# Attention value products: the column halves of the array hold two softmax rows in place of two halves of the key blocks, and one transpose turns two heads' sums

## Chip, cores and metric

The kernel runs on one core of one Trainium2 chip. The metric is the device time of one execution in microseconds (us), lower is better. Engines are written as in the profile: PE is TensorE (PEld its weight loads), DVE is VectorE, ACT is ScalarE, POOL is GpSimd.

## What is computed

Two layers of a hybrid diffusion backbone over 1024 latent tokens and 256 context tokens of width 1024, all in float32. In each layer one input projection feeds four head groups of four heads of 64 (A: global attention with two key/value heads, B: attention in a band of 128 tokens to each side, with a sink, also two key/value heads, C: an mLSTM, D: attention in a 2-D neighbourhood with a learned bias, four key/value heads). Their outputs are normalised by group, go through one output projection, and a gated MLP follows. The change touches the end of A, B and D alone, the weighted sum of values and its division:

```python
p = jax.nn.softmax(s, axis=-1).astype(vals.dtype)
return jnp.einsum('bkgqs,bksd->bkgqd', p, vals)
...
y = rms_norm(y.reshape(b, t, N_GROUPS, GROUP_WIDTH), g_group.reshape(N_GROUPS, GROUP_WIDTH))
```

## The kernel before

**Stages of a layer.** `phase1` normalises, projects for A and runs attention A (`attn_a`), with the rest of the projections (`pj`, lines 111 to 113) behind it. `attn_d` runs D, with the mLSTM steps as filler, and hands on to `attn_b`, which finishes B, with the first part of the output projection (`o`) as filler. `phase3` does the rest of the output projection and the MLP (`b`).

**Jobs.** A query tile has 128 tokens. `job_a` and `job_b` make one job for each tile and key/value head, so two softmax rows (the two query heads that share it); `job_d` makes one for a pair of tiles and one head, so two rows as well (the two tiles). Layer 0 treats 10 tiles, layer 1 only the 8 latent ones. `run_jobs` interleaves the generator `one` of a job (scores, softmax) with `two` of the jobs before it (products, division), and `pump` puts filler between them. That is the order in which instructions are handed over; a scheduler with a simulated timeline then sets the final order of each engine's queue at compile time, by readiness and by that order.

**Scores and softmax.** In A (`job_a`) scores are made with keys on the partitions, so E (exponentials, written two key blocks at a time at line 1136) can go into the products directly. In B and D (`softmax_rows`) queries are on the partitions, and `weigh` first transposes the probabilities cell by cell (a cell is one row and one key block of 128 keys), four cells to a PSUM tile `pT` (line 976), copied to `PT` by ACT or DVE (lines 982, 980).

**Products.** The values of a key block (128 keys by 64) are the weights, the probabilities stream through. Such a product uses 64 of the array's 128 columns, and it is made in one column half, the next product in the other (`r = HD * half`). In the kernel before, a product streams both rows of a block at once (256 columns), blocks alternate between the halves, and so the sum O (128 x 256) has the even blocks' part in partitions 0 to 63 and the odd blocks' part in 64 to 127. In A this is line 1151 (10 key blocks a job, 2 for context tiles). In `weigh` it is line 965, called for one group of at most four cells, one group after the transposes of the next. Products are float32, and the profile has two records for each, two passes.

**Division.** O is copied to `Os` (lines 1155, 1200, 1339). `finish_y` multiplies each head's 128 x 128 slice with two identities stacked (`self.ii`, 128 x 64, line 1006), which adds the two parts and turns the result to tokens on partitions in one product. Line 999 turns the order of D's denominators (`back`), line 1003 sums A's. Then `rd` (line 1008) and `yu` (line 1010) divide, and `group_norm` writes the result.

Of the kernel before, what the change touches and what calls it, by code (L numbers as in the profile page):

```python
# [7 lines left out]
F32 = mybir.dt.float32  # L8
F32R = mybir.dt.float32r
BF16 = mybir.dt.bfloat16  # L10
AF = mybir.ActivationFunctionType
# [4 lines left out]
P = 128  # L16
# [6 lines left out]
HD = 64  # L23
# [16 lines left out]
    return ap.bitcast(F32)  # L40


NB = (3, 4, 4)

SLOTS = "gwwwwgggwwwwggggwww"
# [2 lines left out]
class Net:  # L48
# [893 lines left out]
    def weigh(self, rows, blocks, V, take):  # L942


        nc = self.nc
        yield
        groups = [[]]
        for b in blocks:
            cells = [(s, b) for s in range(2) if b in rows[s][1]]
            if len(groups[-1]) + len(cells) > 4:  # L950
                groups.append([])
            groups[-1] += cells
        O = None
        late = []

        def products(cells, pt):
            nonlocal O, half
            if O is None:
                O = self.asp.tile([P, 256], F32, tag="O", name="O", bufs=1)
            c = 0  # L960
            while c < len(cells):
                s, b = cells[c]
                n = 2 if c + 1 < len(cells) and cells[c + 1][1] == b else 1
                r = HD * half
                nc.tensor.matmul(O[r:r + HD, s * P:(s + n) * P], V[b], pt[:, c:c + n].rearrange("p s t -> p (s t)"),  # L965
                                 start=(cells is groups[0]), stop=(cells is groups[-1]), skip_group_check=True)
                half = 1 - half
                c += n

        half = 0  # L970
        for cells in groups:
            n = len(cells)
            t = self.asp.tile([P, 4, P], F32, tag="T", name="pT", bufs=2)
            for c, (s, b) in enumerate(cells):
                Pm, col = rows[s]
                nc.tensor.transpose(t[:, c], Pm[:, col[b]:col[b] + P], self.ident)  # L976
            pt = self.ap_.tile([P, 4, P], F32, tag="PT", name="PT", bufs=3)
            self.turn += 1
            if self.turn % 4 == 0:
                nc.vector.tensor_copy(pt[:, 0:n], t[:, 0:n])  # L980
            else:
                nc.scalar.copy(out=pt[:, 0:n], in_=t[:, 0:n])
            late.append((cells, pt))
            if len(late) > 1:
                products(*late.pop(0))
            yield cells is groups[-1]
        yield True
        products(*late.pop(0))
        take(O)
        yield True  # L990

    def finish_y(self, i, grp, Os, den, wp, back=False, sums=None):


        nc = self.nc
        Yt = self.asp.tile([P, 4, P], F32, tag="T", name="Y", bufs=2).rearrange("p a b -> p (a b)")
        Y = Yt[:, 0:256]
        if back:
            nc.tensor.matmul(Yt[:, 256:260], self.back, den, start=True, stop=True)
            den = Yt[:, 256:260]  # L1000
        if sums:
            for h in range(4):
                nc.tensor.matmul(Yt[:, 256 + h:257 + h], sums[h // 2][:, 0, h % 2], self.ones[:, 0:1], start=True, stop=True)
            den = Yt[:, 256:260]
        for h in range(4):
            nc.tensor.matmul(Y[:, h * HD:(h + 1) * HD], Os[h], self.ii, start=True, stop=True)  # L1006
        rd = wp.tile([P, 4], F32, tag="rd", name="rd")
        nc.vector.reciprocal(rd, den)
        yu = wp.tile([P, 256], F32, tag="yu", name="yu", bufs=1)
        nc.vector.tensor_tensor(out=yu.rearrange("p (h d) -> p h d", d=HD), in0=Y.rearrange("p (h d) -> p h d", d=HD),  # L1010
                                in1=rd.unsqueeze(2).broadcast_to([P, 4, HD]), op=ALU.mult)
        self.group_norm(yu, i, grp, wp)

    def attn_pools(self, st, name, side, q_bufs, qt_bufs):
        p = {"qp": self.sb(st, name + "q", bufs=q_bufs, side=side), "wp": self.sb(st, name + "w", bufs=2, side=side)}
        p["ii"] = p["wp"].tile([P, HD], F32, name="ii", bufs=1)
        self.nc.sync.dma_start(p["ii"], self.a["ii"])
        p["ap_"] = self.sb(st, name + "p", side=side)
        p["qt_bufs"] = qt_bufs
        return p  # L1020
# [72 lines left out]
    def job_a(self, i, kv, t, KS, VS, fetch, prep):  # L1093

        nc = self.nc
        blocks = range(2 if i < 2 else NT)
        n = len(blocks)

        def one():
# [33 lines left out]
            for b in range(0, n, 2):  # L1133
                e = E[:, b:b + 2]
                nc.vector.tensor_tensor(out=e, in0=e, in1=T[:, 2:4].unsqueeze(1).broadcast_to([P, 2, 2, P]), op=ALU.subtract)
                nc.scalar.activation(out=e, in_=e, func=AF.Exp)
                if b:
                    nc.gpsimd.tensor_tensor(D, E[:, 0:2] if b == 2 else D, e, ALU.add)
                yield
# [5 lines left out]
        def two():  # L1145
            E = t["E", kv]
            yield
            O = self.asp.tile([P, 256], F32, tag="O", name="O", bufs=1)
            for b in blocks:
                r = HD * (b % 2)  # L1150
                nc.tensor.matmul(O[r:r + HD], VS[:, b, kv], E[:, b].rearrange("p h t -> p (h t)"),  # L1151
                                 start=(b < 2), stop=(b >= n - 2), skip_group_check=True)
            if kv == 0:
                t["Os"] = self.wp.tile([P, 4, P], F32, tag="Os", name="Os", bufs=1)
            nc.scalar.copy(out=t["Os"][:, 2 * kv:2 * kv + 2], in_=O.rearrange("p (s t) -> p s t", s=2))
            yield True
            if kv:
                self.finish_y(i, 0, [t["Os"][:, h] for h in range(4)], None, self.wp, sums=t["ds"])
                yield True
        return dict(one=one, two=two)  # L1160

    def job_b(self, i, kv, t, KS, VS, mask, sink, fetch, prep):
# [33 lines left out]

        def take(O):
            if kv == 0:
                t["Os"] = self.wp.tile([P, 4, P], F32, tag="Os", name="Os", bufs=1)
            nc.scalar.copy(out=t["Os"][:, 2 * kv:2 * kv + 2], in_=O.rearrange("p (s t) -> p s t", s=2))  # L1200

        def two():
            yield from self.weigh(t["rows", kv], blocks, {b: VS[:, b, kv] for b in blocks}, take)
            if kv:
                den = t["den"]
                nc.vector.tensor_tensor(out=den, in0=den, in1=t["es"], op=ALU.add)
                self.finish_y(i, 1, [t["Os"][:, h] for h in range(4)], den, self.wp)
                yield True
        return dict(one=one, two=two)

# [76 lines left out]
    def job_d(self, pair, h, t, KS, VS, EP, EI, fetch, prep):  # L1287
# [21 lines left out]

        def one():  # L1310
            if h == 0:
                for s in range(2):
                    t["den", s] = self.wp.tile([P, 4], F32, tag=f"den{s}", name="den")
            if h == 1:
                fetch((pair[0] + 2, pair[0] + 3))
            if h == 3:
                prep((pair[0] + 2, pair[0] + 3))
            t["rows", h] = []
            for s in range(2):
                r0, nr, bias = info[s]  # L1320
                chunks = [(K[:, 0:NCTX], None)]
                if nr:
                    n = nr * HD // 2
                    bf = bias.rearrange("p a b -> p (a b)")
                    for c in range(2):
                        k0 = NCTX + r0 * HD + c * n
                        chunks.append((K[:, k0:k0 + n], bf[:, c * n:(c + 1) * n]))

                def after(Pm, nm, nr=nr):
                    if nr == 9:  # L1330
                        nc.gpsimd.memset(Pm[:, 832:896], 0.0)

                Pm = yield from self.softmax_rows(chunks, (*t["q"][s], h), 3.0e38, t["den", s][:, h:h + 1], 896, after)
                t["rows", h].append((Pm, cols[s]))

        def take(O):
            if h == 0:
                t["Os"] = self.wp.tile([P, 4, 2, P], F32, tag="Os", name="Os", bufs=1)
            nc.scalar.copy(out=t["Os"][:, h], in_=O.rearrange("p (s t) -> p s t", s=2)[:, :, ::-1])

        def two():
            yield from self.weigh(t["rows", h], blocks, {b: VS[:, b, h] for b in blocks}, take)
            if h == 3:
                for s in range(2):
                    self.finish_y(pair[s], 3, [t["Os"][:, x, s] for x in range(4)], t["den", s], self.wp, True)
                    yield True
        return dict(one=one, two=two)


# [320 lines left out]
def constants():  # L1670
# [1 line left out]
    c = {}  # L1672
    c["ident"] = np.eye(P, dtype=f)
    c["back"] = np.ascontiguousarray(np.eye(P, dtype=f)[::-1])
    c["ii"] = np.concatenate([np.eye(HD, dtype=f)] * 2)
    s8 = np.zeros((P, 8), f)
    for g in range(4):
        for v in range(2):
# [62 lines left out]
```

## Time and profile before

| what | value |
|---|---|
| median of three runs | 3477.2 us (3476.16 to 3477.77) |
| the profiled execution's own time | 3473.32 us |
| its span in the trace | 3471.6 us |
| mean granted TensorE clock | 0.976 |
| busy, share of the span | PE 96%, PEld 78%, DVE 63%, ACT 43%, POOL 28% |
| matmul records | 19629 |

The span is the time from the first to the last instruction of the profiled execution; the own time has what lies around it too. Busy shares are means over stages that differ. A matmul's record is longer than the time after which the next one may start, since matmuls are pipelined: what a matmul costs is read from one start to the next.

### The profile page before, as it was taken

How to read it: one execution, taken by the hardware profiler on the slowest of the kernel's cores; microseconds unless marked ns; L12 is line 12 of the kernel's file. 1: busy time of each engine (PE TensorE's matmuls, PEld its weight loads, DVE VectorE, ACT ScalarE, POOL GpSimd, SP SyncE). 2: the span in 40 equal slices, each digit the busy share in tenths (PEclk: the TensorE clock that was granted, in tenths of full speed). 3: DMA queues.
4: the chain of work that ended last, by engine and by line, in shares of the span. 5: the costliest groups of instructions: out<-in, count | busy, mean ns of one | idle time of the engine just before them, and what ended most of it. 6: DMA issues, size and time to landing. Idle time of an engine off the chain costs nothing. (4 is left out here: it accounts for less than half of the span.)

```text
span 3471.6 us, 52832 instructions
## 1 busy us (share of the span) xinstructions
PE 3332.2 (96%) x19629; PEld 2698.5 (78%) x19629; DVE 2178.5 (63%) x4103; ACT 1498.5 (43%) x3005; POOL 967.1 (28%) x1069
## 2 busy tenths in 40 slices
PE   7999999999988999999999999999999889999998
PEld 4777877777867888888888678877778668888887
DVE  4545553775457778778454736654763588888745
ACT  4334423566544444444120535434564444444321
POOL 1524333232353222220000623424222543322000
PEclk8999999999998999999999999999999989999999
DMA  7645145315321222216222543156233222222521
GB/s 281 184 133 170 41 118 152 87 59 173 125 81 58 73 66 65 74 60 221 75 83 73 160 162 101 44 139 153 60 127 108 83 73 76 91 76 103 195 84 61
DMA packets 393897, 377.52 MB, mean 109 GB/s; under 512 B 118184, under 2 KB 335400, under 8 KB 387496
## 3 DMA queue, kind: packets, MB, share of 16 engines
q1 hardware_dynamic: 393640, 374.15, 34.1%
q8 instruction: 155, 2.54, 0.3%
q14 instruction: 102, 0.84, 0.1%
HBM read 279.69 MB, written 94.37 MB: 108 GB/s over the span
## 5 line engine op out<-in xcount | busy, mean ns | idle before, releaser
L112 PE MATMUL b<-g,w 128*128 128x512 f32 (+1 forms) x880 | 321.9, 368 | 0.0
L113 PE MATMUL b<-g,w 128*128 128x512 f32 (+1 forms) x880 | 320.8, 368 | 0.0
L111 PE MATMUL b<-g,w 128*128 128x512 f32 (+1 forms) x880 | 320.1, 368 | 0.0
L1638 DVE SCALAR_TENSOR_TENSOR xT<-b,modT,xT 128x512 f32<-128x512 f32 (+1 forms) x280 | 191.5, 695 | 202.9 <-PE b L113 202.3
L111 PE MATMUL pj<-whi,hh 128*128 128x512 f32 (+2 forms) x800 | 282.0, 355 | 16.9 <-ACT v L528 7.1
L112 PE MATMUL pj<-wlo,hh 128*128 128x512 f32 (+2 forms) x800 | 281.5, 353 | 2.8 <-DVE wlo L103 2.7
L113 PE MATMUL pj<-whi,hl 128*128 128x512 f32 (+2 forms) x800 | 278.2, 350 | 0.0
L1512 POOL TENSOR_TENSOR s<-raw 128x512 f32<-128x512 f32 x88 | 120.0, 1363 | 466.1 <-DVE w L1519 387.5
L111 PEld LDWEIGHTS pj<-whi,hh 128*128 128x128 f32 x800 | 153.3, 192 | 52.2 <-ACT v L528 11.1
L111 PEld LDWEIGHTS b<-g,w 128*128 128x128 f32 x880 | 165.5, 189 | 27.8
L112 PEld LDWEIGHTS b<-g,w 128*128 128x128 f32 x880 | 165.6, 189 | 27.4
L113 PEld LDWEIGHTS b<-g,w 128*128 128x128 f32 x880 | 165.3, 188 | 27.6
L112 PEld LDWEIGHTS pj<-wlo,hh 128*128 128x128 f32 x800 | 153.9, 193 | 32.1 <-DVE wlo L103 7.6
L1518 ACT CAST w<-s 128x512 fp32r<-128x512 f32 x176 | 107.0, 618 | 153.2 <-PE b L113 101.9
L113 PEld LDWEIGHTS pj<-whi,hl 128*128 128x128 f32 x800 | 153.7, 192 | 23.5 <-issue 4.7
L1541 DVE SCALAR_TENSOR_TENSOR cg<-u,vec,cg 128x512 f32<-128x512 f32 (+1 forms) x176 | 166.2, 988 | 9.1 <-ACT cg L1536 9.1
L86 ACT CAST w<-raw 128x512 fp32r<-128x512 f32 x88 | 53.7, 619 | 270.5 <-PE b L113 244.1
L1519 DVE TENSOR_TENSOR w<-raw,w 128x512 fp32r<-128x512 f32 x154 | 132.7, 875 | 53.3 <-ACT w L1518 50.3
L112 PE MATMUL o<-yl,wohi 128*128 128x256 f32 x576 | 164.9, 287 | 0.7 <-DVE yl L87 0.7
L113 PE MATMUL o<-yh,wolo 128*128 128x256 f32 x576 | 165.0, 288 | 0.0
L111 PE MATMUL o<-yh,wohi 128*128 128x256 f32 x576 | 164.7, 288 | 0.2
L103 POOL TENSOR_TENSOR wolo<-raw,wohi 128x512 fp32r<-128x512 f32 x80 | 103.9, 1300 | 162.6 <-ACT wohi L102 158.0
(364 smaller groups left out, 9769.4 us busy)
## 6 DMA issues: line engine op xcount, KB each, us to landing
wmod<-in_w_mod_dram SPq DMA_DIRECT2D x48, 1024.0 KB, 6.5
raw<-in_w_up_dram SPq DMA_DIRECT2D x176, 256.0 KB, 2.9
raw<-in_w_down_dram SPq DMA_DIRECT2D x88, 256.0 KB, 4.6
raw<-in_w_in_dram SPq DMA_DIRECT2D x80, 256.0 KB, 4.2
raw<-in_w_out_dram SPq DMA_DIRECT2D x80, 256.0 KB, 3.3
sG<-cv SPq DMA_DIRECT2D x22, 640.0 KB, 3.3
graw<-sG SPq DMA_DIRECT2D x22, 640.0 KB, 5.1
sG<-cv SPq DMA_DIRECT2D x22, 512.0 KB, 4.1
```

The source lines that it names most:

```text
L86: nc.scalar.copy(out=hi, in_=src)
L103: eng.tensor_tensor(lo[:, 0:w], raw[:, 0:w], f32v(hi[:, 0:w]), ALU.subtract)
L111: nc.tensor.matmul(out, lh, rh, start=(first and i == 0), stop=False, **kw)
L112: nc.tensor.matmul(out, lh, rl, start=False, stop=False, **kw)
L113: nc.tensor.matmul(out, ll, rh, start=False, stop=(last and i == n - 1), **kw)
L1512: nc.gpsimd.tensor_tensor(s, x, y, op)
L1518: nc.scalar.copy(out=hi, in_=src)
L1519: nc.vector.tensor_tensor(out=lo, in0=src, in1=f32v(hi), op=ALU.subtract)
L1541: nc.vector.scalar_tensor_tensor(out=o[:, x0:x1], in0=u[:, x0 - d - c:x1 - d - c], scalar=self.cw[w][:, j:j + 1], in1=o[:, x0:x1], op0=ALU ...
L1638: nc.vector.scalar_tensor_tensor(out=xs, in0=o[:, 0:t1 - t0], scalar=modT[:, 40 + f, v:v + 1], in1=xs, op0=ALU.mult, op1=ALU.add)
```

## The change

A product now streams one row of one block (128 columns), the first row into partitions 0 to 63 and the second into 64 to 127, so O is 128 x 128 and each half holds a complete sum. In A, one more thing is new: the first product of a job is made to wait for the last exponential of that job (`add_manual_dep`). In `weigh`, cells are cut in fours across blocks, the products of two groups are issued together after the transposes of a third, the rest at the end, and `PT` has four buffers, not three. `finish_y` transposes a pair of heads at a time; for D the new `finish_pair` transposes one head of both tiles at a time, into one PSUM tile for the two, and takes a second tile of the same ring for the denominators. The division itself is moved to `divide`, unchanged. The constant `ii` and its loads are gone.

```diff
 # weigh
-        groups = [[]]
-        for b in blocks:
-            cells = [(s, b) for s in range(2) if b in rows[s][1]]
-            if len(groups[-1]) + len(cells) > 4:
-                groups.append([])
-            groups[-1] += cells
+        cells = [(s, b) for b in blocks for s in range(2) if b in rows[s][1]]
+        ends = [[c for c in cells if c[0] == s] for s in range(2)]
+        ends = {x[0] for x in ends}, {x[-1] for x in ends}
+        groups = [cells[g:g + 4] for g in range(0, len(cells), 4)]
...
-        def products(cells, pt):
-            nonlocal O, half
+        def products(groups):
+            nonlocal O
             if O is None:
-                O = self.asp.tile([P, 256], F32, tag="O", name="O", bufs=1)
-            c = 0
-            while c < len(cells):
-                s, b = cells[c]
-                n = 2 if c + 1 < len(cells) and cells[c + 1][1] == b else 1
-                r = HD * half
-                nc.tensor.matmul(O[r:r + HD, s * P:(s + n) * P], V[b], pt[:, c:c + n].rearrange("p s t -> p (s t)"),
-                                 start=(cells is groups[0]), stop=(cells is groups[-1]), skip_group_check=True)
-                half = 1 - half
-                c += n
+                O = self.asp.tile([P, P], F32, tag="O", name="O", bufs=1)
+            for cells, pt in groups:
+                for c, x in enumerate(cells):
+                    r = HD * x[0]
+                    nc.tensor.matmul(O[r:r + HD], V[x[1]], pt[:, c], start=(x in ends[0]), stop=(x in ends[1]),
+                                     skip_group_check=True)
...
-            pt = self.ap_.tile([P, 4, P], F32, tag="PT", name="PT", bufs=3)
+            pt = self.ap_.tile([P, 4, P], F32, tag="PT", name="PT", bufs=4)
...
-            if len(late) > 1:
-                products(*late.pop(0))
+            if len(late) > 2:
+                products(late[:2])
+                late = late[2:]
             yield cells is groups[-1]
         yield True
-        products(*late.pop(0))
+        products(late)
         take(O)
 # finish_y
-        Y = Yt[:, 0:256]
-        if back:
-            nc.tensor.matmul(Yt[:, 256:260], self.back, den, start=True, stop=True)
-            den = Yt[:, 256:260]
+        for p in range(2):
+            nc.tensor.transpose(Yt[:, p], Os[:, p], self.ident)
...
-        for h in range(4):
-            nc.tensor.matmul(Y[:, h * HD:(h + 1) * HD], Os[h], self.ii, start=True, stop=True)
+    def finish_pair(self, pair, grp, Os, den, wp):
+        nc = self.nc
+        Yt = self.asp.tile([P, 4, P], F32, tag="T", name="Y", bufs=2).rearrange("p a b -> p (a b)")
+        for h in range(4):
+            nc.tensor.transpose(Yt.rearrange("p (s h d) -> p h s d", s=2, h=4)[:, h], Os[:, h], self.ident)
+        dt = self.asp.tile([P, 4, P], F32, tag="T", name="dT", bufs=2)
+        nc.tensor.matmul(dt[:, 0, 0:8], self.back, den, start=True, stop=True)
+        for s in range(2):
+            self.divide(pair[s], grp, Yt[:, 256 * s:256 * s + 256], dt[:, 0, 4 * s:4 * s + 4], wp)
 # job_a
-                nc.scalar.activation(out=e, in_=e, func=AF.Exp)
+                t["exp", kv] = nc.scalar.activation(out=e, in_=e, func=AF.Exp)
...
-            O = self.asp.tile([P, 256], F32, tag="O", name="O", bufs=1)
+            O = self.asp.tile([P, P], F32, tag="O", name="O", bufs=1)
+            first = True
             for b in blocks:
-                r = HD * (b % 2)
-                nc.tensor.matmul(O[r:r + HD], VS[:, b, kv], E[:, b].rearrange("p h t -> p (h t)"),
-                                 start=(b < 2), stop=(b >= n - 2), skip_group_check=True)
+                for h in range(2):
+                    r = HD * h
+                    m = nc.tensor.matmul(O[r:r + HD], VS[:, b, kv], E[:, b, h], start=(b == 0), stop=(b == n - 1),
+                                         skip_group_check=True)
+                    if first:
+                        self.tc.add_manual_dep(m.ins, t["exp", kv].ins.name, SYNC, reason="all products in one run")
+                    first = False
...
-            nc.scalar.copy(out=t["Os"][:, 2 * kv:2 * kv + 2], in_=O.rearrange("p (s t) -> p s t", s=2))
+            nc.scalar.copy(out=t["Os"][:, kv], in_=O)
 # job_d
-            nc.scalar.copy(out=t["Os"][:, h], in_=O.rearrange("p (s t) -> p s t", s=2)[:, :, ::-1])
+            nc.scalar.copy(out=t["Os"][:, h], in_=O[:, ::-1])
...
-                for s in range(2):
-                    self.finish_y(pair[s], 3, [t["Os"][:, x, s] for x in range(4)], t["den", s], self.wp, True)
-                    yield True
+                self.finish_pair(pair, 3, t["Os"], t["den"], self.wp)
+                yield True
```

## Rows read from the trace of the kernel before

**Rows 1.** Page, busy time by engine (share of the span, records).

```profile
PE 3332.2 (96%) x19629; PEld 2698.5 (78%) x19629; DVE 2178.5 (63%) x4103; ACT 1498.5 (43%) x3005; POOL 967.1 (28%) x1069
```

**Rows 2.** Busy us by stretch, sum of 158 to 456 and 2012 to 2267 (A).

```profile
sum 553.00, PE 549.51 PEld 437.88 DVE 308.06 ACT 246.05 POOL 201.18; mean PE 274.75 PEld 218.94 DVE 154.03 ACT 123.03 POOL 100.59
```

**Rows 3.** Same view, sum of 594 to 754 and 2390 to 2545 (D).

```profile
sum 315.00, PE 311.54 PEld 238.64 DVE 235.34 ACT 182.85 POOL 95.69; mean PE 155.77 PEld 119.32 DVE 117.67 ACT 91.42 POOL 47.84
```

**Rows 4.** Same view, sum of 754 to 901 and 2545 to 2657 (B).

```profile
sum 259.00, PE 253.48 PEld 191.91 DVE 146.90 ACT 175.09 POOL 55.52; mean PE 126.74 PEld 95.95 DVE 73.45 ACT 87.55 POOL 27.76
```

**Rows 5.** Waits, total us, times, longest: ACT in A, DVE in D (layer 0).

```profile
ACT E L1117 <- PE S L1116: 60.6, 40, 4.1
...
DVE Pm L931 <- PE S L930: 11.0, 17, 1.6
```

**Rows 6.** O: records, ns min/median/max, starts, forms; what PE idled for (us, times).

```profile
L965 PE MATMUL O<-PT,vs x784: 272/379/689, 594.0 to 2653.0; 128*64 128x256 f32 x180, 128*64 128x128 f32 x16
L1151 PE MATMUL O<-E,vs x656: 379/379/431, 171.1 to 2267.1; 128*64 128x256 f32 x164
...
  ACT E L1136: 1.9, 5
```

**Rows 7.** Timeline of PE in A: start us, us, instruction.

```profile
2173.15 0.28 PE L111 MATMUL pj<-hh,whi 128*128 128x256 f32 x1
2173.26 0.28 PE L112 MATMUL pj<-hl,whi 128*128 128x256 f32 x1
2173.47 1.95 PE L1151 MATMUL O<-E,vs 128*64 128x256 f32 x16
2175.35 0.38 PE L113 MATMUL pj<-hh,wlo 128*128 128x256 f32 x1
2175.58 0.28 PE L111 MATMUL pj<-hh,whi 128*128 128x256 f32 x1
```

**Rows 8.** Timeline of PE: first and last of A's 131 runs of products.

```profile
171.08 0.65 PE L1151 MATMUL O<-E,vs 128*64 128x256 f32 x4
171.66 0.44 PE L1127 MATMUL mT<-ident,M 128*128 128x128 f32 x2
...
2266.81 0.65 PE L1151 MATMUL O<-E,vs 128*64 128x256 f32 x4
```

**Rows 9.** Timeline of PE: first and last of the 207 runs in D and B.

```profile
594.04 0.98 PE L965 MATMUL O<-PT,vs 128*64 128x256 f32 x4
...
2652.76 0.65 PE L965 MATMUL O<-PT,vs 128*64 128x256 f32 x4
```

**Rows 10.** Timeline of PE: a pair of 128-column products; a 256-column product without partner.

```profile
671.89 0.44 PE L965 MATMUL O<-PT,vs 128*64 128x128 f32 x4
672.26 0.66 PE L976 MATMUL pT<-ident,Pm 128*128 128x128 f32 x4
...
883.94 0.65 PE L965 MATMUL O<-PT,vs 128*64 128x256 f32 x2
884.52 0.66 PE L976 MATMUL pT<-ident,Pm 128*128 128x128 f32 x4
```

**Rows 11.** Records that write or read Y, columns as in the group on O.

```profile
L1006 PE MATMUL Y<-ii,Os x432: 217/275/472, 182.6 to 2656.5; 128*128 128x64 f32 x144
L999 PE MATMUL Y<-den,back x36: 168/253/274, 618.2 to 2552.1; 128*128 128x4 f32 x36
...
L1010 DVE TENSOR_TENSOR yu<-Y,rd x54: 410/424/426, 186.4 to 2656.8; 128x256 f32<-128x256 f32 x54
```

**Rows 12.** Timeline of PE: one tile's eight Y records; two transposes.

```profile
430.55 1.08 PE L1006 MATMUL Y<-ii,Os 128*128 128x64 f32 x8
431.44 0.36 PE L1115 MATMUL S<-QH,ks 128*128 128x256 f32 x1
...
180.82 0.38 PE L1127 MATMUL mT<-ident,M 128*128 128x128 f32 x2
181.03 0.28 PE L1003 MATMUL Y<-ones,D 128*128 128x1 f32 x2
```

## Prediction before the run

> **What bounds the kernel now.** I read the page first: PE is busy 96% of the span [rows 1]. That alone says little, so I cut the span into the stretches that hold the products. In A (553 us over both layers) PE is busy for 549.5 us, in D for 311.5 of 315, in B for 253.5 of 259, while DVE stands at 308, 235 and 147 us and ACT at 246, 183 and 175 [rows 2 to 4]. The waits say the same: ACT stands 60.6 us in layer 0's A for scores that PE has not made, DVE 11.0 us in D [rows 5]. In these three stretches the queue of PE sets the pace, so what counts is how long each PE instruction holds up the next. That is read from starts in the timeline.
>
> **What a run of products costs.** I call products that follow one another in PE's queue a run. A run of 16 records takes 1.88 us to the next instruction [rows 7], one of 4 records 0.58 us [rows 8]. Records come in pairs, one in each column half, so 6 more pass pairs cost 1.30 us: 0.217 us for a pass pair of 256 columns. With 128 columns, 4 records take 0.37 us [rows 10], 0.105 us less for each pass pair, so 0.112 us. The rest is paid once a run. Inside it: 1.88 - 8 x 0.217 = 0.14 us. Ahead of it: O starts 0.21 us after the projection before it, where projections follow each other after 0.11 us, so 0.10 us. Behind it: the second projection comes 0.23 us after the first, so 0.11 us more. Together **0.35 us for each run**, however long.
>
> **Products of A.** Before: 656 records [rows 6] are 328 pass pairs x 0.217 = 71.2 us, and 131 runs [rows 8] x 0.35 = 45.9 us: 117.1 us. Each run is short because exponentials land two key blocks at a time, and the scheduler puts each two products where their exponentials are ready. After: twice the products, each of 128 columns, the two rows of a block in the two halves: 656 pass pairs x 0.112 = 73.5 us. The new wait lets none start before all inputs are there. There are 18 tiles x 2 = 36 jobs, so 36 runs if none is broken. I take 45, as instructions handed over earlier can become ready in mid-run: 15.8 us. The gain is 117.1 - 89.3 = **27.8 us**.
>
> **The wait in A.** The first product now waits for the job's last exponential, and scores of the next job and projections are queued behind it on PE. Now PE idles 1.9 us for exponentials, 5 times [rows 6]. At worst each of 36 jobs waits as long (0.4 us): 14 us; at best nothing, and the 1.9 us are won. I take 2 us, since the queue's order is made for the new wait too. The sum O is done later: 20 pass pairs x 0.112 = 2.2 us behind the last exponential, where the last 4 records took 0.58 us. That delays `Os`, Y and the release of E by 1.7 us; PE has projections to fill it, so I price it at nothing. Without them it would be 36 x 1.7 = 60 us.
>
> **Products of D and B.** Before: 784 records in 207 runs [rows 6, 9]. The code makes 208 groups of cells (48 + 44 in B, 60 + 56 in D), so a group was a run and hardly one was broken. Of the products, 24 are the last two cells of a B job with five key blocks: a 256-column product with no partner, which takes the 0.58 us of a full pair [rows 10]. So 336 pass pairs of 256 columns, 48 such passes alone, 32 pass pairs of 128 columns: 384 x 0.217 + 32 x 0.112 = 86.9 us, and 207 x 0.35 = 72.5 us. After: 752 cells, one pass pair each: 84.2 us. By the code B has 60 runs and D 68 (two groups together, then the rest); I take 63 and 72, so 47.3 us. The gain is 159.4 - 131.5 = **27.9 us**: 14.0 in D, 13.9 in B.
>
> **Turning the sums.** `finish_y`'s 432 records [rows 11] take 0.89 us for a tile's eight [rows 12], 0.111 us each, 48.0 us. After: one transpose for each pair of heads and tile, 108, at 0.21 / 2 = 0.105 us [rows 12], say 0.11: 11.9 us. That is a gain of **36 us**, 12 each in A, B and D. The `back` products halve from 36 records [rows 11] to 18: 2 us.
>
> **Edits priced at nothing.** `Os` copies become half as wide; ACT is not the bound. The fourth `PT` and the loss of `ii` and of its six loads cost no engine time. `divide` is as it was. `finish_pair` holds both tiles of the ring that transposes use through two divisions, nine times: each has 0.42 us of `yu` [rows 11] and as much again at most for the rest, so from nothing to 9 x 1.7 = 15 us. I take nothing by itself, because scores and mLSTM steps do not use that ring; it is one reason for the discount below.
>
> **The sum.** PE is freed of 39.9 us in A, 28.1 in D and 26.0 in B: 94.0 us. In A nothing else is near its limit (DVE 56%), so all but the 2 us of waits shorten the span: 38. In D, DVE would rise from 75% to 235 / 287 = 82%, in B ACT from 68% to 175 / 233 = 75% [rows 3, 4], with chains of dependent steps through both. There I count 80%: 22.5 + 20.8 us. That makes 81 us: 3392 against the profiled execution's own 3473.3 us (span 3471.6), and, as the median of the runs lies 3.9 us above it, **3396 us** as the forecast.
>
> **A rule against it.** The six further pass pairs of the long run add only their columns: 256 columns cost 0.217, 128 cost 0.112, so with 0.105 us for each 128 columns some 0.007 us are left over, and the weight loads of passes after the first are hidden [rows 7, 8, 10]. The Trainium skill ("TensorE: Matmul & The Clock Gate", Part 3, The mechanism) says that a weight load overlaps running matmuls only where the row groups differ; both column halves share them, so each pass would pay its load, an estimated 53 ns for 64 columns by the same page. By that rule the 1408 pass pairs after would cost 75 us more, and the sum would be some 3460 us. The runs of 256 columns here speak against the rule. No row shows a third pass of 128 columns, in which a load has half the time to hide.
>
> **Rivals.** (1) *DVE in D and ACT in B become the bound* and half of the 54 us there is lost: 3477.2 - 38 - 27 = 3412 us. For it: the chains and the shared ring. Against it: both mostly wait for PE today [rows 5]. (2) *The runs stay short.* The scheduler's simulated time knows no price of 0.35 us, so it may put other work between products, and 338 runs remain. Only turning (38 us) is gained: at nine tenths 3442 us. Against it: where products were ready together, 207 runs came of 208 groups. (3) *Slower: loads show in every 128-column pass.* Place: the second half of each run. At most the 0.14 us inside a run is such a load, paid by 1408 pass pairs: 205 us, so 3477 - 81 + 205, about 3600 us. It decides from 81 / 1408 = 58 ns a pass; above, the kernel is slower. Against it: 0.007 us left over above, and the 0.37 us of the four-record run has room for one load only.
>
> **How the numbers follow.** Forecast 0.62, rival 1 0.17, rival 2 0.11, rival 3 0.05 (half of it at a price below 58 ns, still faster), and 0.05 for an order of the queues that costs otherwise. The low end: all 94 us, another 6 for unbroken runs (16 x 0.35), and half of the 12.6 us that PE idles in the three stretches: 3371 us. The high end takes in rivals 1 and 2: 3442 us. About 0.2% is what a measurement of this kernel tells from no change. Faster by more: 0.94; within: 0.02; slower: 0.04.
>
> **What would show it.** Right: products of 128 columns alone, some 180 runs; long runs in A with 0.22 us for two pass pairs; Y with 108 transposes 0.11 us apart; A 38 us shorter over both layers, D and B 20 us each; PE still the busiest in all three. Rival 1: the same PE rows, but PE idle in D behind DVE or in B behind ACT. Rival 2: about as many runs as now. Rival 3: pass pairs more than 0.15 us apart. The forecast is wrong if A does not shorten though its runs did, or if PE waits for exponentials by tens of us.

## Result, and the profile after

The change made the kernel faster, by far less than forecast: 3448.17 us median (3444.78 to 3449.32) against 3477.48 us for the kernel before on the same chip, a ratio of 0.9912 (95% interval 0.9897 to 0.9927). A second measurement in a later session gave 3451.95 us, ratio 0.9927 (0.9914 to 0.9941). That is a gain of 25 to 31 us where 81 were forecast, and outside the range. The profiled execution took 3447.27 us with a span of 3445.1 us, at a mean granted clock of 0.972.

The page's busy time by engine, after (before: [rows 1]):

```profile
PE 3273.5 (95%) x20663; PEld 2734.2 (79%) x20663; DVE 2175.4 (63%) x4103; ACT 1485.1 (43%) x3005; POOL 963.3 (28%) x1069
```

PE is busy for 59 us less, yet the span is only 26.5 us shorter. More than half of what PE was freed of has become idle time: 139.4 us before, 171.6 after. The products and transposes after, from the groups by tile (columns as in [rows 6, 11]):

```profile
L962 PE MATMUL O<-PT,vs x1504: 272/273/477, 575.3 to 2623.8; 128*64 128x128 f32 x188
L1158 PE MATMUL O<-E,vs x1312: 272/273/476, 163.5 to 2221.4; 128*64 128x128 f32 x188
...
L993 PE MATMUL Y<-ident,Os x72: 270/272/477, 173.3 to 2626.8; 128*128 128x128 f32 x72
L1006 PE MATMUL Y<-ident,Os x36: 270/273/329, 598.6 to 2523.7; 128*128 128x128 f32 x36
```

All products have 128 columns, 2816 records or 1408 pass pairs, and 72 + 36 = 108 records turn the sums in place of 432. So the change does what it says. Its unit prices are in the timeline of PE (start us, us, instruction), which also shows the place where the time is lost:

```profile
163.55 0.66 PE L1158 MATMUL O<-E,vs 128*64 128x128 f32 x8
164.13 0.39 PE L114 MATMUL pj<-hh,wlo 128*128 128x256 f32 x1
...
2219.30 2.40 PE L1158 MATMUL O<-E,vs 128*64 128x128 f32 x40
2221.63 0.39 PE L112 MATMUL pj<-whi,hh 128*128 128x256 f32 x1
...
2233.16 1.05 PE L621 MATMUL gt<-ident,gates 128*10 128x128 f32 x8 [0.21 <-DVE X L623]
2252.18 0.44 PE L661 MATMUL tp<-ident,ends 10*4 10x10 f32 x8 [17.98 <-DVE ends L653]
...
2257.85 0.58 PE L113 MATMUL pj<-wlo,hh 128*128 128x256 f32 x1 [3.64 <-DVE wlo L104]
...
2264.14 1.87 PE L711 MATMUL tk<-sel,cum 42*128 42x20 f32 x8
...
2402.45 0.66 PE L962 MATMUL O<-PT,vs 128*64 128x128 f32 x8
```

A job's 40 records of A stand in one run and take 2221.63 - 2219.30 = 2.33 us to the next instruction, 8 records take 0.58 us. So 16 more pass pairs cost 1.75 us, 0.109 us each (forecast 0.112). In D and B most runs are still of 8 records, one group of four products. The four rows from `gt` on are the surprise: between the last transposes of the mLSTM's gates (`gt`) and the transposes of the scans' ends (`tp`) PE does nothing for 18 us, then waits 3.6 us more for a weight. In the kernel before, projections stood there and `tp` did not wait, as its own timeline shows at the same place:

```profile
2293.45 1.05 PE L620 MATMUL gt<-ident,gates 128*10 128x128 f32 x8
2294.43 0.50 PE L113 MATMUL pj<-whi,hl 128*128 128x512 f32 x1
...
2309.12 0.39 PE L112 MATMUL pj<-wlo,hh 128*128 128x512 f32 x1
2309.44 0.26 PE L660 MATMUL tp<-ident,ends 10*4 10x10 f32 x8
```

Busy us by stretch, after. The three sums are A, D and B as in [rows 2 to 4]. Then come four stretches, with columns: from and to, length, busy us of PE, PEld, DVE, ACT and POOL with their records, granted clock, DMA share, GB/s. They are A with the passage up to D's first product, then D and B with the output projection up to the MLP's first product `b`, for layer 0 and layer 1. The last three rows are the idle time of layer 1's passage and what follows it.

```profile
sum 529.00, PE 521.66 PEld 465.93 DVE 313.11 ACT 241.40 POOL 204.39; mean PE 260.83 PEld 232.96 DVE 156.55 ACT 120.70 POOL 102.19
...
sum 307.00, PE 303.38 PEld 247.25 DVE 234.03 ACT 180.17 POOL 92.37; mean PE 151.69 PEld 123.62 DVE 117.01 ACT 90.09 POOL 46.18
...
sum 246.00, PE 234.28 PEld 194.61 DVE 146.79 ACT 167.68 POOL 55.51; mean PE 117.14 PEld 97.31 DVE 73.40 ACT 83.84 POOL 27.75
...
154.00:575.00 421.00, 402.24 (x3098) 345.14 (x3096) 213.36 (x413) 163.16 (x347) 149.59 (x174) 0.98 0.42 127
575.00:986.00 411.00, 398.31 (x3282) 334.04 (x3281) 243.27 (x798) 240.64 (x629) 133.99 (x192) 0.99 0.39 116
1980.00:2372.00 392.00, 366.13 (x2859) 324.09 (x2859) 202.81 (x397) 152.94 (x315) 146.19 (x170) 0.95 0.37 107
2372.00:2724.00 352.00, 343.82 (x2805) 285.10 (x2803) 203.72 (x671) 198.56 (x503) 99.23 (x153) 0.98 0.36 108
...
2233.00:2252.00 19.00, 1.05 (x8) 0.69 (x8) 15.24 (x25) 5.07 (x6) 9.44 (x8) 0.65 0.71 161
2252.00:2273.00 21.00, 16.63 (x71) 14.79 (x72) 10.97 (x26) 4.81 (x7) 0.00 (x0) 0.50 0.32 103
2273.00:2290.00 17.00, 16.81 (x75) 13.56 (x73) 4.25 (x5) 3.58 (x5) 0.00 (x0) 1.00 0.45 120
```

The same four stretches of the kernel before:

```profile
158.00:594.00 436.00, 426.27 (x2819) 336.16 (x2817) 209.75 (x413) 165.68 (x348) 149.30 (x174) 0.99 0.40 122
594.00:1014.00 420.00, 412.10 (x3036) 327.47 (x3035) 247.60 (x799) 245.94 (x627) 134.86 (x192) 0.99 0.38 114
2013.00:2392.00 379.00, 370.55 (x2549) 302.12 (x2548) 201.91 (x394) 155.17 (x313) 145.78 (x168) 1.00 0.37 108
2392.00:2750.00 358.00, 352.47 (x2567) 276.47 (x2566) 204.21 (x673) 201.85 (x503) 101.17 (x155) 1.00 0.35 106
```

A alone became 24 us shorter (553 to 529), where 38 were forecast. With the passage behind it, A's two stretches went from 815 to 813 us: layer 0 won 15, layer 1 lost 13. PE's busy time in them fell from 796.8 to 768.4 us, and its idle time rose from 18.2 to 44.6. D and B with the output projection went from 778 to 763 us. The wait itself, in the profile's list of waits after (total us, times, longest), is the largest of PE; the list of before has no wait of `tp` for the scans:

```profile
PE tp L661 <- DVE ends L653: 26.6, 2, 18.0
```

### The profile page after: what moved, and what is told of

Its sections match the earlier page's. It is cut to its first block, busy times and chain, and to the rows that moved or that the text cites. A ratio compares the mean times of both kernels' runs of the same rounds, so it can differ in the third digit from the quotient of the medians.

```text
span 3445.1 us, 54930 instructions
## 1 busy us (share of the span) xinstructions
PE 3273.5 (95%) x20663; PEld 2734.2 (79%) x20663; DVE 2175.4 (63%) x4103; ACT 1485.1 (43%) x3005; POOL 963.3 (28%) x1069
```

## The experiments

**The theory** is that the products and transposes cost what was forecast, and that two things took the gain back. One is the passage from A to D: after the change PE's queue holds no projections between `gt` and `tp` in layer 1, so DVE's scans show. The other is D and B, where the runs did not grow long, since no wait holds a job's first group for the second. The rivals are named in the expectations: above all that the new wait in A holds PE up, or that another engine is the bound. Ratios are to the kernel before on the same chip. The counts below are of the queue of PE as compiled; the traces show the same numbers:

```
kernel           runs A   runs D and B   projections between gt and tp, layer 1   ratio
before             131        207                    57                            1
after               36        195                     0                       0.9912, 0.9927
e_fill              36        200                    52                          0.9862
e_weighdep          36        137                     0                          0.9879
e_both              36        138                    52                          0.9805
e_nowait            82        195                     0                          0.9936
e_bwait             36        205                    58                          0.9936
e_bfill            131        207                    57                          0.9994
e_turn              82        203                    63                          0.9892
e_more              36        138                    52                          0.9796
e_prime             36        138                    52                          0.9816
e_queue             36        199                     0                          0.9901
```

**Projections handed over earlier (e_fill).** The projections of chunk C2 are handed over between the mLSTM's steps, not after them, so that the scheduler has something to put under the scans.

```diff
...
+            c2 = steps(C_C2)
             for us in self.ml:
                 if us is None:
                     break
+                for _ in range(int(us * 1.5)):
+                    next(c2, None)
...
-            run(C_C2, C_B)
+            for _ in c2:
+                pass
+            run(C_B)
```

> The changed kernel, with the first steps of the projection chunk C2 handed over between the steps of the mLSTM's preparation, so that projections stand in PE's queue between the gate transposes and the product that waits for the scans. Theory P (part of the gain was lost in the passage from A to D, because PE's queue had nothing to do there while DVE scanned: 18.0 us in layer 1, 9.0 in layer 0): both waits fall under 3 us and the median falls by 18 to 26 us from 3448, to some 3426. Rival R (the chain scans, mLSTM start, D sets that passage, whatever PE does): the waits go, D starts no earlier, and the median stays within 5 us of 3448.

Measured: 3425.9 us, ratio 0.9862 (0.9847 to 0.9877), span 3421.8. From its timeline, and the two stretches of A with the passage:

```profile
2248.08 0.44 PE L671 MATMUL tp<-ident,ends 10*4 10x10 f32 x8 [5.99 <-DVE ends L663]
...
2268.39 1.04 PE L721 MATMUL tk<-sel,cum 42*128 42x20 f32 x8
```

```profile
153.00:568.00 415.00, 401.83 (x3108) 346.59 (x3106) 213.29 (x415) 163.91 (x349) 150.45 (x175) 0.98 0.43 130
...
1974.00:2348.00 374.00, 362.64 (x2853) 319.44 (x2853) 201.72 (x397) 153.41 (x315) 146.19 (x170) 0.98 0.39 113
```

The wait fell from 18.0 to 6.0 us, A with the passage from 813 to 789 us (421 to 415, 392 to 374). The median came as the theory said. The waits fell by less than it said: 6.0 us in layer 1 and 4.2 in layer 0 are left, not under 3.

**The same on the kernel before (e_bfill).** A control: does the edit gain by itself? (The last lines of the edit, as above, are left out.)

```diff
+            c2 = steps(C_C2)
...
+                for _ in range(int(us * 1.5)):
+                    next(c2, None)
```

> The kernel before, with the same edit at the mLSTM's preparation as the first run (steps of chunk C2 between its steps). A control. Theory P (the kernel before has projections in that place anyway, 57 products in either layer as its queue is compiled, so the 18 us are a loss that came with the change): within 6 us of the kernel before. Rival C (the edit gains some 20 us on any kernel, and so says nothing of where the change's gain went): 15 us faster or more.

Measured: 3474.94 us, ratio 0.9994 (0.9985 to 1.0003). By itself it gains nothing (it even brings 4.8 us of waits at `tp`, where the kernel before has none); the roughly 20 us that e_fill is faster than the kernel after are time that the change had lost.

**The same wait in `weigh` (e_weighdep).** The first product of a call with two groups waits for the second group's copy.

```diff
...
+                    if first and len(groups) > 1:
+                        self.tc.add_manual_dep(m.ins, groups[-1][2].ins.name, SYNC, reason="both groups in one run")
...
-                nc.scalar.copy(out=pt[:, 0:n], in_=t[:, 0:n])
-            late.append((cells, pt))
+                cp = nc.scalar.copy(out=pt[:, 0:n], in_=t[:, 0:n])
+            late.append((cells, pt, cp))
```

> The changed kernel, with the same kind of wait in weigh that the change has in A: the first product of a call waits for the last probability copy of that call. Theory P (the runs in D and B stayed short, 195 where 135 were forecast, because the first group's products were ready before the second group's): some 140 runs, 55 fewer, at about 0.3 us each 16 us of PE, and the median falls by 10 to 18 us to some 3434. Rival R (in D and B DVE and ACT set the pace): 140 runs too, but PE idles instead, and the median stays within 5 us of 3448.

Measured: 3432.47 us, ratio 0.9879 (0.9866 to 0.9893). A run in layer 1's D, where the last timeline row of the kernel after had 8 records, and its two stretches of D and B with the output projection:

```profile
2403.23 1.09 PE L963 MATMUL O<-PT,vs 128*64 128x128 f32 x16
```

```profile
576.00:977.00 401.00, 388.31 (x3285) 333.97 (x3284) 244.59 (x799) 239.95 (x628) 133.61 (x192) 0.99 0.40 119
...
2362.00:2709.00 347.00, 335.65 (x2810) 284.18 (x2809) 204.44 (x675) 197.67 (x505) 100.49 (x156) 1.00 0.37 110
```

Two groups now mostly stand in one run, 137 runs in all, where the prediction had 135. D and B with the output projection take 748 us, not 763. Layer 1's wait at `tp` stayed at 18.3 us: the two losses are separate.

**Both edits (e_both).**

```diff
+            c2 = steps(C_C2)
...
+                    if first and len(groups) > 1:
+                        self.tc.add_manual_dep(m.ins, groups[-1][2].ins.name, SYNC, reason="both groups in one run")
```

> Both edits of the two runs before. Theory P: the gains add up, 28 to 44 us, a median of some 3412. Rival R: within 8 us of 3448.

Measured: 3405.59 us, ratio 0.9805 (0.979 to 0.9821): about 68 us (0.0195 x 3476), 13 short of the forecast's 81. The two gains add up as the theory said.

**Without the wait in A (e_nowait).** The rival: the wait is itself the loss.

```diff
-            first = True
+            first = False
             for b in blocks:
```

> The changed kernel without the wait for the last exponential in A. Theory P: the runs in A are broken again (some 80 for 36), 46 more at about 0.3 us, and the wait of PE for the scans in layer 1 stays near 18 us, so the median rises by 8 to 16 us to some 3460. Rival W (it is the new wait that pulled the projections ahead and emptied PE's queue at the scans): the 18 us go, and the median falls to some 3442 in spite of the shorter runs.

Measured: 3455.08 us, ratio 0.9936 (0.9924 to 0.9949), slower than the kernel after by 3 to 8 us, less than the 8 to 16 of the theory, and the intervals of the two overlap. A has 82 runs; `tp` in layer 1 still waits 17.7 us, so the rival falls there. In layer 0 `tp` does not wait any more, but projections ahead of it wait 7.1 and 6.4 us for their weights.

**Only the wait, on the kernel before (e_bwait).**

```diff
...
+                if b == 0:
+                    self.tc.add_manual_dep(m.ins, t["exp", kv].ins.name, SYNC, reason="all products in one run")
```

> The kernel before, with only the wait in A: the first product (256 columns, halves of the key blocks as before) waits for the job's last exponential. 36 runs for 131 in A. Theory P (a run costs some 0.3 us of PE however long, and the queue of this kernel keeps its projections between the gate transposes and the scans' reader): 95 runs less, 28 us of PE, so 22 to 30 us faster than before. Rival (the cost of a run is hidden under other work, the gain of the change is the turning of the sums): under 8 us faster.

Measured: 3455.0 us, ratio 0.9936 (0.9923 to 0.9948), some 22 us, the low end of the theory. A's 10 products of 256 columns stand in one run:

```profile
2026.26 2.38 PE L1152 MATMUL O<-E,vs 128*64 128x256 f32 x20
2028.57 0.44 PE L1128 MATMUL mT<-ident,M 128*128 128x128 f32 x2
```

They take 2.31 us to the next instruction, as the 40 records of 128 columns take 2.33. So A's unbroken runs do not need the new halves (though without the wait the changed kernel has 82 runs and not 131): with one such wait most of the change's net gain is had. The passage is covered all the same. Its rows in layer 1, and the two stretches of A with the passage:

```profile
2277.22 1.05 PE L621 MATMUL gt<-ident,gates 128*10 128x128 f32 x8
2278.20 0.50 PE L112 MATMUL pj<-whi,hh 128*128 128x512 f32 x1
...
2293.43 0.26 PE L661 MATMUL tp<-ident,ends 10*4 10x10 f32 x8
```

```profile
157.00:580.00 423.00, 409.65 (x2822) 338.46 (x2820) 212.67 (x413) 165.10 (x348) 150.58 (x174) 0.98 0.42 126
...
1997.00:2366.00 369.00, 362.12 (x2547) 307.76 (x2546) 198.97 (x393) 152.32 (x311) 143.11 (x165) 0.98 0.38 109
```

A with the passage became 23 us shorter here (815 to 792), and 57 and 58 projections still lie between `gt` and `tp` in the two layers, with no wait at `tp`. So a shorter A does not by itself empty the passage.

**Without the two steps that make runs long (e_turn).** The change with e_fill, but without the wait in A and with one group at a time: mainly what the halves and the turning are worth.

```diff
-            if len(late) > 2:
-                products(late[:2])
-                late = late[2:]
+            if len(late) > 1:
+                products(late[:1])
+                late = late[1:]
...
-            first = True
+            first = False
```

> The changed kernel without its longer runs: no wait in A, in weigh one group of cells at a time as before, and with the steps of chunk C2 between the preparation's steps. What is left of the change is the two rows in the two halves and the turning by transposes. By its queue as compiled it has 82 runs in A and 203 in D and B. Theory P (turning frees 38 us of PE, rows in halves 4 in B, fewer runs some 14; three quarters of that shorten the time): 36 to 46 us faster than before, a ratio near 0.988. Rival T (the Y products were beside other work; nearly all of the change's gain is in the runs): less than 20 us faster.

Measured: 3437.98 us, ratio 0.9892 (0.9879 to 0.9906), 38 us, inside the theory's range. It equals the forecast's 38 for turning and `back`, but that is in part luck: the run also has 53 runs fewer than the kernel before (285 for 338), and what each is worth was not separated. With the wait in A (e_fill) 48, with long runs in D and B as well (e_both) 68.

**More of the filler (e_more, e_prime).** Two tries at the 10 us that `tp` still waits in e_both: more steps of C2, and C2's weights handed over before the gates, each an edit of e_both.

```diff
-                for _ in range(int(us * 1.5)):
+                for _ in range(int(us * 2.5)):
```

> Both edits, with more steps of chunk C2 between the preparation's steps (2.5 for each unit in place of 1.5). Theory P: the waits of PE for the scans that were left (6.3 us in layer 1, 4.6 in layer 0) shrink below 2 us and the median falls by 3 to 9 us more. Rival R: DVE's scans come later by what is handed over ahead of them, and the median stays within 3 us of that of both edits.

```diff
             c2 = steps(C_C2)
+            next(c2)
...
-                for _ in range(int(us * 1.5)):
+                for _ in range(int(us * 2)):
```

> Both edits of the third run, with the weights and the first step of chunk C2 handed over ahead of the gate transposes. Theory P (what is left of PE's wait for the scans, 5.9 us in layer 1 and some 4 in layer 0, comes from the casts of these weights in DVE's queue ahead of the scans): those waits fall below 2 us and the ratio to before is 0.0015 to 0.003 lower than the third run's 0.9805. Rival: the waits stay, within 0.0015.

Measured: 3407.42 us, 0.9796 (0.9782 to 0.9809), and 3411.11 us, 0.9816 (0.9802 to 0.9829). Both theories missed, and the times are the rivals': the waits at `tp` stayed at 9.4 and 10.3 us, and e_both took as long.

**Where the late weights come in (e_queue).** In the kernel after, the last two of C1's eight weight slices are also late. SP's queue issues them only behind D's keys (`kD`) and bias (`ep`), as the timeline of SP after shows (they are the first of the six in its last row):

```profile
2224.02 1.01 SPq L97 DMA_DIRECT2D raw<-in_w_in_dram  x2
...
2232.91 10.10 SPq L1292 DMA_DIRECT2D ep<-in_rpb_pad_dram  x15
2243.11 16.30 SPq L97 DMA_DIRECT2D raw<-in_w_in_dram  x6
```

A projection needs all eight, so this could be the cause. The edit puts the loads of `kD` and `ep` into ACT's queue, and the weights then stand ahead.

```diff
-                        nc.sync.dma_start(k[x * HD:(x + 1) * HD], self.sD_qk[4 + h])
+                        nc.scalar.dma_start(k[x * HD:(x + 1) * HD], self.sD_qk[4 + h])
...
-                    nc.sync.dma_start(EP[h][64 - 64 * rr:128 - 64 * rr, 7 * b:7 * b + 7], src)
+                    nc.scalar.dma_start(EP[h][64 - 64 * rr:128 - 64 * rr, 7 * b:7 * b + 7], src)
```

> After, with the loads of kD and ep (D's keys and bias, 20 transfers a layer) on ACT's DMA queue instead of SP's. In the kernel after, SP issues the last two of C1's eight weight slices in layer 1 only at 2243 us, behind 4 kD and 16 ep loads, and PE's queue has no projection between the gates (gt) and the scans' ends (tp). With this edit the weight slices stand in front, while PE's queue still has no projection between gt and tp in layer 1. Theory Q (the order of PE's queue makes the 18 us wait; the late weights cost only what PE waits for wlo behind it): the wait of tp stays 17 to 19 us, the 3.6 us for wlo go, the median is 0 to 6 us under the kernel after (3442 to 3451). Rival L (the late weights make it): the wait of tp falls to 7 us or less and the median to some 3425 to 3430, as with the filler handed over early.

Measured: 3439.71 us, ratio 0.9901 (0.9884 to 0.9917). In its timeline:

```profile
2224.10 3.25 PE L621 MATMUL gt<-ident,gates 128*10 128x128 f32 x32
2248.70 0.44 PE L661 MATMUL tp<-ident,ends 10*4 10x10 f32 x8 [21.35 <-DVE ends L653]
...
2253.65 0.58 PE L113 MATMUL pj<-wlo,hh 128*128 128x256 f32 x1 [2.92 <-DVE wlo L104]
```

The wait stays, at 21.4 us, so the order of SP's queue is not its cause: with no projection between `gt` and `tp` in PE's queue, PE waits. The wait for `wlo` (3.6 us in after) was expected to go, and 2.9 us are left. The gain over the kernel after is small and the intervals overlap; in the traces it lies in layer 0, where `tp` waits 1.7 us (23.1 in all, 21.4 of it in layer 1) and not 8.6.

## Why the prediction was wrong

**The prices.** A pass pair of 128 columns cost 0.109 us (forecast 0.112), and the Y transposes took 11.5 us (forecast 11.9). I also summed each run's time over the timeline, from the start of the instruction ahead to the second one behind, less the usual spacing of those two. A's 36 runs took 88.4 us, where 89.3 was forecast for 45 (before: 124.7, where 117.1 was forecast). But taking a run away gave back less than the 0.35 us it was priced at: 95 runs fewer made A with the passage 23 us shorter in e_bwait and PE's busy time there 25 us less, and 58 fewer than after made D and B 15 us shorter in e_weighdep. That is about 0.25 us a run. This term was too high.

**The rule did not hold.** A pass pair of 256 columns took 0.217 us [rows 7, 8]; one of 128 columns, with weights of its own for each half, took 0.109 us in a long run, half as much, so nothing is left over for a load. Loads are hidden here though both halves share their rows. The Trainium skill ("TensorE: Matmul & The Clock Gate", Part 3, The mechanism) says that a load overlaps running matmuls only where row groups differ; the trace disagrees with "only", and the measurement decides. The same section of the Trainium skill also lets a load run ahead where it goes to a background weight buffer; no run here tells what hid these loads. The kernel before already had a sign of this that the prediction did not use for it: two transposes, each with weights of 128 columns on the same rows, take 0.21 us [rows 12], 0.105 each, which is just what the prediction counts for 128 columns without a load. Rival 3 falls with the rule: it decided from 0.058 us a pass. (The prediction's sum by the rule has a slip: 3396 + 75 is 3471, not 3460.)

**The step that failed first:** "In A nothing else is near its limit (DVE 56%), so all but the 2 us of waits shorten the span: 38." PE was indeed freed: its busy time in A with the passage fell by 28.4 us, though it includes work at the slow clock. But the stretch won 2 us, not 38. The busy share of DVE was the wrong evidence. What mattered is a chain: `gt`, steps of ACT, DVE's two scans and their ends, `tp`. From the last `gt` to `tp` it takes 15 to 22 us in these traces, in which PE needs other work. In the kernel before 57 projections lay there in either layer. After the change the scheduler, which fixes the queue's order at compile time, left none for layer 1's passage and 33 for layer 0's. It is shown that the cover was lost with the change, and that putting it back returns most of the time; which part of the change moved the projections is not shown. The wait in A is not it (e_nowait), and neither is a shorter A by itself (e_bwait). The prediction asked what hides the edits it priced at nothing, but not whether the cover further back would stay.

The wait cost more than its 18 us. After it the granted clock stands at 0.50, the 1.2 GHz level, through 16.6 us of busy time up to 2273 us, in the last row but one of the stretches above. The eight `tk<-sel,cum` records take 1.87 us there and 1.04 in e_fill. So an estimated 16.6 x (1 - 1.04 / 1.87) = 7.4 us went to the clock: with the 18.0 and the 3.6 us some 29 us in layer 1, and 8.6 (26.6 - 18.0) more at layer 0's `tp`.

**The second step that failed:** "By the code B has 60 runs and D 68 (two groups together, then the rest); I take 63 and 72, so 47.3 us." There were 195 runs, not 135. The products of the first group are ready before the second group's copy, so the scheduler puts them alone. This was rival 2, true in D and B and false in A, and it shows what made the difference: the written wait. Priced as a whole with one chance, it could not come out half. With the wait (e_weighdep) there are 137 runs, and the runs of D and B take 128.0 us, against 145.2 after and 155.5 before. The forecast for after was 131.5.

**The share of 80% in D and B** was too high, and so was what it was taken of. The sum freed PE of 54 us there. In e_weighdep, with long runs, PE's busy time in those stretches is 724 us, 41 under the 764.6 of before, and the stretches are only 30 us shorter (778 to 748), 73% of it: the idle time rose from 13.4 to 24.0. By the list of PE's waits in these stretches, those for transfers rose from 2.1 to 7.1 us (B's keys and queries above all), those for DVE from 5.9 to 10.0, those for ACT from 4.7 to 5.1. So rival 1 explains a few us of it. PE stays the busiest engine (303.4 of 307 us in D after).

**The sum, again.** The change as it is: 28 us, the middle of its two ratios. Most of the passage's loss returned (e_fill): 48. Long runs in D and B as well (e_both): 68. The forecast: 81. The last 13 us stay open. Three things are of that size: the 10.1 us of waits at `tp` in e_both, which two tries did not remove; the lower share in D and B; and the price of a run, an estimated 0.1 us too high for each of the 164 runs that went (338 to 174), 16 us. I have not told them apart. Open too is by what rule the scheduler ordered layer 1's passage as it did. Some 9 us of the span's gain lie outside the four stretches (26.5 - 17); they were not followed.

## What to carry to other kernels

A freed engine's gain is only as good as the cover further down its queue: look for chains of another engine (here DVE's scans) that the work hides today, and look in the new queue at what lies under them after the edit. Where a compile-time scheduler makes the order, unbroken runs come from a written wait and not from handing instructions over together: one such wait on the old kernel won 22 us. After an edit, compare stretches that include the passage to the next stage, with PE's busy and idle time apart; A alone showed a gain of 24 us, of which 2 were left with the passage behind it.

## What the runs showed of the hardware that I had not expected

The price of an idle gap goes on after it: 18 us of idle PE were followed by 16.6 us of busy time at a granted clock of 0.50, and in e_fill, after a wait of 6.0 us, the clock was at 0.54 for 6 us and back at 1.00 when the same records ran, in 1.04 us and not 1.87. After e_queue's wait of 21.4 us, longer than the 18 us, the clock was 0.62 over the next 21 us, so the price does not simply grow with the gap. The rows of e_fill, then that of e_queue:

```profile
2248.00:2254.00 6.00, 5.92 (x22) 4.74 (x23) 0.95 (x6) 0.54 (x2) 1.13 (x1) 0.54 0.65 193
2254.00:2270.00 16.00, 16.00 (x91) 13.30 (x89) 5.51 (x15) 4.03 (x8) 0.00 (x0) 1.00 0.18 67
...
2249.00:2270.00 21.00, 17.53 (x85) 15.46 (x83) 11.87 (x26) 4.37 (x6) 0.00 (x0) 0.62 0.48 143
```

The Trainium skill ("TensorE: Matmul & The Clock Gate", Part 1, What's actually happening) says that the slow level is the state of an idle engine, and that activity releases it; the rows of after agree, 0.50 after the gap and 1.00 further on.

Two products of 128 columns in the two halves, with their own weights each, cost what one product of 256 columns costs (2.33 us for 40 records, 2.31 for 20): twice the loads cost nothing that shows.
